# Last attention group finished in halves of its columns, squares of the last two token parts summed on TensorE, order of the last projections and scalings written out by hand

## The chip, the cores and the metric

The kernel runs on one core of one Trainium2 chip. The metric is the device time of one execution in microseconds (us). The engines are named as in the profile: PE is TensorE's matmuls, PEld its weight loads, DVE is VectorE, ACT is ScalarE, POOL is GpSimd, SP is SyncE, which here issues the DMAs. A line such as L1396 is a line of the kernel before; the changed kernel has other line numbers, and its lines stand in the order listings and the diff only.

## The reference

Two layers of a diffusion backbone run over 1024 latent tokens of width 1024, with 256 context tokens ahead of them in the first layer. The first layer is two kinds of grouped attention; the second is a convolution branch beside a neighbourhood attention with a bias table. What this change touches is the end of the second layer: the last heads of the neighbourhood attention, their gate, the output projection, the gated residual, and the final normalization.

```python
def rms_norm(x, g):
    xf = x.astype(jnp.float32)
    y = xf * lax.rsqrt(jnp.mean(xf * xf, axis=-1, keepdims=True) + EPS)
    return (y * g.astype(jnp.float32)).astype(x.dtype)
...
    y_lat = jnp.concatenate([oc, od * jax.nn.silu(dg)], axis=-1) @ w_out     # odd layer
...
        x_lat = x_lat + g_l[:, None, :] * y_lat
...
    return rms_norm(x_lat, final_g)
```

## The kernel before

**Layout.** Everything is held transposed: a tile has 128 channels on its partitions and tokens along its columns. A 1024-channel stream is therefore eight blocks, e = 0 to 7. The latent tokens are dealt into two halves of 512 (hf = 0 and 1). A value that enters a projection is held as a high part and a low part, both in the rounded float type fp32r, and one product is three matmuls into the same PSUM bank: high by high, low by high, high by low (`mm3`, L319, L320, L321). The function `split` makes the two parts: ACT casts the high part (L297), DVE or POOL subtracts (L300).

**Attention of the second layer.** Sixteen groups run one after the other, each one head (hd) over one half of the tokens (hf). A group ends in `attn_gen.flush`: the bank `ov` holds the head's weighted values in partitions 0 to 63 and the softmax denominators in partitions 64 to 127. DVE transposes the denominators of the two halves of 256 columns into `r1` (L421), takes reciprocals (L423), transposes them back and so spreads them (L424), and calls `finish`: two multiplies of 64x256 (L1329), one with the gate over 64x512 (L1331), and for the last head pair the split into `od3`, whose two parts are the moving operands of the last projections (L297 on ACT, L300 on DVE).

**Output projection.** It is accumulated in parts. Channels from the convolution and the first heads are added into `x2[hf]` while the attention still runs. What is left for the end are three token parts, listed in `ENDS`: part 0 is all 512 tokens of half 0, part 1 columns 0 to 255 of half 1, part 2 columns 256 to 511 of half 1. For each part `out1_end(k)` goes through the eight blocks: the matmuls of the last heads (for parts 1 and 2 only the last head pair, f = 7, so one `mm3` of 256 columns), the eviction into x2 with the gated residual on DVE (L1396), and a square on ACT (L1425). In the kernel before the squares of all eight blocks are then added up into two tiles of 128 tokens by columns, on DVE or, where `SQP` says so, on POOL (L1429); for part 2 the two tiles are added (L1432).

**Final norm.** `rstd_steps` sums over the partitions with matmuls whose stationary operand is the summed squares and whose moving operand is a column pair of 1/1024 (`ones`; L252, two per 128 tokens and tile in the program, each of them two passes in the trace). Then come a scalar step on DVE (L255), a power on POOL (L239), three small steps on DVE (L240 to L242), and a matmul against the identity that spreads the result over all partitions (`bc`, L262). `final_norm(k)` scales the eight blocks: those listed in `FNP[k]` by ACT (gain, L1444) and POOL (L1445, from a copy of `bc` that ACT makes, L1440), the others by one DVE instruction (L1447). After each second block SP issues a DMA to the output (L1449).

**Order.** Every engine takes its instructions strictly in the order written. That order is set when the kernel is built, by a scheduler with priorities that goes by the order in which the Python code emits the work. Up to the last group, the ends are woven between attention steps (`weave`). After it, `run(ends(EVS))` emits part 1, its rstd, part 2, norm 1, rstd 2, norm 2, and the scheduler interleaves them. `BUFS` gives the PSUM banks; after the attention (`solo`) projections rotate over four banks (two of `pp`, two of `mx`), so the fifth projection waits until the first was evicted.

Of the kernel before, what the change touches and what calls it, by code (L numbers as in the profile page):

```python
# [56 lines left out]
WV = (73, 53, 77, 24, 12)  # L57
SQ = (0, 1)
EV0 = "e0 c0 f0".split()
EVS = "e1 c1 e2 f1 c2 f2".split()  # L60
NEV = 30
ADDS = (0, 0, 1)
# [26 lines left out]
def tile_kernel(ctx: ExitStack, tc: tile.TileContext, a, out):  # L89
# [152 lines left out]
        VE.scalar_tensor_tensor(r[:, :n], t[:, :n], 1.5, r[:, :n], op0=ALU.add, op1=ALU.mult)  # L242
        return r

    def rstd_steps(pool, accs, n, tag, inv=1.0, tr="tr"):


        nb = n // P
        tr = bank(tr, nm("trs"))
        for b in range(nb):  # L250
            for k, acc in enumerate(accs):
                PE.matmul(tr[:, 2 * b : 2 * b + 2], acc[:, b * P : (b + 1) * P], ones, start=(k == 0),  # L252
                          stop=(k == len(accs) - 1))
        v = pool.tile([P, 8], F32, tag="rbv", name=nm("rbv"), bufs=2)
        VE.tensor_scalar(v[:, :nb], tr[:, 0 : 2 * nb].rearrange("p (b two) -> p b two", two=2)[:, :, 0],  # L255
                         inv, EPS, op0=ALU.mult, op1=ALU.add)
        r = newton_rsqrt(pool, v[:, :nb], nb, "rb")
        yield
        yield
        bc = bank(tag, nm("bc"))  # L260
        for b in range(nb):
            PE.matmul(bc[:, b * P : (b + 1) * P], r[:, b : b + 1].broadcast_to([P, P]), ident, start=True, stop=True)  # L262
        return bc
# [130 lines left out]
    def attn_gen(pool, groups, vshare, look, nexts=None):  # L394
# [6 lines left out]
        def flush():  # L401
            g, t, ph, pl = pend.pop(0)
            k, q0, n, _ = g.tiles[t]
            if t == 0:
                g.ov = bank("ov", nm("ov"))
                if g.load_v is not None:
                    g.load_v()
            V = g.v(k)
            last = t == len(g.tiles) - 1
            o = g.ov[:, q0 : q0 + n]  # L410
            PE.matmul(o, V[:, 64:192], ph[:, :n], start=(t == 0), stop=False)  # L411
            PE.matmul(g.ov[0:64, q0 : q0 + n], V[:, 0:64], ph[:, :n], start=False, stop=False)  # L412
            pvs.append(PE.matmul(o, V[:, 64:192], pl[:, :n], start=False, stop=(last and g.sink is None)))  # L413
            if last:
                if g.sink is not None:
                    PE.matmul(g.ov, g.skm(), g.QL[0:76, :], start=False, stop=True)
                r1 = pool.tile([P, 8, 32], F32, tag="r1", name=nm("r1"), bufs=1)
                r8 = pool.tile([P, 8], F32, tag="r8", name=nm("r8"), bufs=2)
                rb = pool.tile([P, 256], F32, tag="rb", name=nm("rb"), bufs=1)
                for e in range(2):  # L420
                    VE.transpose(r1[e * 64 : (e + 1) * 64].rearrange("p a b -> p (a b)")  # L421
                                 .rearrange("p (a q) -> p a q", a=2), g.den(g.ov[64:128, :], e))
                VE.reciprocal(r8, r1[:, :, 0])  # L423
                VE.transpose(rb, r8[:, :, None].broadcast_to([P, 8, 32]))  # L424
                g.finish(g.ov, rb)
# [638 lines left out]
    with ExitStack():  # L1064
# [193 lines left out]
        def group1(gi, hd, hf):  # L1258
# [66 lines left out]
            def finish(ov, rb):  # L1325
                fin[0] += 1
                y = half("y1")
                for k in range(2):
                    VE.tensor_tensor(y[ds, k * 256 : (k + 1) * 256], ov[0:64, k * 256 : (k + 1) * 256],  # L1329
                                     rb[k * 64 : (k + 1) * 64, :], op=ALU.mult)  # L1330
                VE.scalar_tensor_tensor(y[ds], y[ds], 0.5, g.gt[ds], op0=ALU.mult, op1=ALU.mult)  # L1331
# [76 lines left out]

        def out1_end(k):

            hf, o, n = ENDS[k]
            accs = []
            for e in range(DK):
                if k == 0:
                    if e % 2 == 0:
# [3 lines left out]
                    yield from out1((7,), e, hf, *wend[e // 2], o, n)  # L1419
                x = x2[hf][:, e, o : o + n]  # L1420
                if k:
                    sq = dpool.tile([P, 512], F32, tag="ph" if e in SQ else "pl", name=nm("sq2"), bufs=LOOK1 + 1)[:, :n]
                else:
                    sq = half("sq2", "hf") if e in SQ else pair("sqt", 512, "vT")[:, 0].bitcast(F32)
                SC.activation(sq, x, AF.Square)  # L1425
                if e in SQ:
                    accs.append(sq)
                else:
                    (GP if e in SQP[k] else VE).tensor_tensor(accs[e % 2], accs[e % 2], sq, op=ALU.add)  # L1429
                yield  # L1430
            if ADDS[k]:
                VE.tensor_tensor(accs[0], accs[0], accs[1], op=ALU.add)  # L1432
                accs = accs[:1]
            sums[k] = accs

        def final_norm(k, bc):
            hf, o, n = ENDS[k]
# [17 lines left out]
        def ends(evs):  # L1455
            for ev in evs:
# [1 line left out]
                if ev[0] == "e":  # L1458
                    yield from out1_end(k)
                elif ev[0] == "c":  # L1460
                    bcs[k] = yield from rstd_steps(dpool, sums[k], ENDS[k][2], BCT[k])
                else:
                    yield from final_norm(k, bcs[k])

# [128 lines left out]
```

## Time and profile before

| what | value |
|---|---|
| runs | 1596.81, 1595.64, 1587.97 us; median 1595.64 us |
| profiled execution, its own time | 1590.95 us |
| its span (first to last instruction) | 1589.2 us, so 1.75 us lie around it |
| mean granted TensorE clock | 0.965 |
| busy share | PE 92%, PEld 74%, DVE 71%, ACT 48%, POOL 52% |
| last matmul of the last group (`ov`) ends | 1554.4 us after the start of the span |
| from there to the end of the span | 34.8 us, of which PE is busy 17.86, DVE 24.59, ACT 9.88, POOL 17.50 |

All times inside the span are counted from its start. A row of stretches gives, for each engine, the busy time and the number of instructions, and after them the granted TensorE clock (1.00 is full speed). In a row of the timeline stand the start, the length, the engine, the line, the operation and its operands; several equal instructions in a row are merged, with xN behind them. Matmuls are pipelined: the length of one is more than the distance to the next.

### The profile page before, as it was taken

To read this page: it belongs to the slowest core of one execution; us is meant where nothing else is said; L and a number is where in the kernel's file an instruction comes from. 1 tells how busy PE (TensorE), PEld (TensorE's weight loads), DVE (VectorE), ACT (ScalarE), POOL (GpSimd) and SP (SyncE) were. 2 spreads that over 40 slices of the span, in tenths; PEclk is the share of its full clock that TensorE was granted. 3 is DMA by queue.
4 is the path that set the end of the run, shared out by engine and by line. 5 is a ranking of instruction groups with operands and counts; after the bars stand their busy time and mean duration, and the time that the engine had idled before them with its cause. 6 is when DMAs were issued, how large, how long until landed. Compare 5 with 4: busy or idle time off the path is not lost.

```text
span 1589.2 us, 22236 instructions
## 1 busy us (share of the span) xinstructions
PE 1459.0 (92%) x6984; PEld 1180.6 (74%) x6984; DVE 1124.1 (71%) x2172; ACT 756.6 (48%) x1542; POOL 831.3 (52%) x760
## 2 busy tenths in 40 slices
PE   6789989998999988989999889999999999789895
PEld 1779867787778667767887768888887787577685
DVE  4898787588857668455478776999846467576676
ACT  2722353444434664654555564443433455545473
POOL 1561364455636667756654655754532334444575
PEclk9999999998999999989999989999999999799997
DMA  9548234532442123471111122213456878888732
GB/s 316 179 144 270 83 101 138 176 95 80 146 143 75 36 65 113 156 223 51 57 40 44 57 66 79 92 55 107 162 176 219 246 222 262 239 219 232 221 97 106
DMA packets 198462, 222.01 MB, mean 140 GB/s; under 512 B 18812, under 2 KB 154696, under 8 KB 198344
## 3 DMA queue, kind: packets, MB, share of 16 engines
q1 hardware_dynamic: 191680, 209.02, 42.9%
q10 hardware_dynamic: 6664, 11.57, 2.4%
q8 instruction: 55, 0.90, 0.2%
q14 instruction: 63, 0.52, 0.1%
HBM read 160.49 MB, written 60.03 MB: 139 GB/s over the span
## 4 chain that ended last, share of the span: by engine, by line
PE 61%; DVE 15%; DMA 13%; issue 4%; POOL 3%; SPq 2%; ACT 1%; DVEq 0%; POOLq 0%; ACTq 0%
PE p L320 6%; PE p L319 6%; PE p L321 6%; PE ov L411 4%; PE ov L413 4%; PE ov L412 3%; PE po L320 3%; PE po L319 3%; PE po L321 3%; PE st L448 3%; PE st L452 3%; DMA mw<-in_mod_w_dram 3%; DMA QH<-QD 2%; PE pq L321 2%; PE pq L319 2%
## 5 line engine op out<-in xcount | busy, mean ns | idle before, releaser
L300 POOL TENSOR_TENSOR pl<-pf,ph 128x512 fp32r<-128x512 f32 (+4 forms) x321 | 394.1, 1239 | 304.4 <-ACT ph L297 252.4
L300 POOL TENSOR_TENSOR wl<-wr,wh 128x256 fp32r<-128x256 f32 (+2 forms) x256 | 199.3, 794 | 218.2 <-ACT wh L297 209.4
L460 ACT ACTIVATE pf<-st 128x512 f32<-128x512 f32 x284 | 166.2, 596 | 171.3 <-PE st L452 126.5
L297 ACT CAST ph<-pf 128x512 fp32r<-128x512 f32 (+4 forms) x364 | 209.9, 588 | 38.4 <-PE ov L412 22.0
L297 ACT CAST wh<-wr 128x256 fp32r<-128x256 f32 (+2 forms) x264 | 103.4, 404 | 162.4 <-DMA wr<-in_od_d_dram 38.6
L319 PE MATMUL p<-hh,wh 128*128 128x512 f32 x448 | 177.2, 397 | 2.4 <-DVE spk L300 1.4
L320 PE MATMUL p<-hl,wh 128*128 128x512 f32 x448 | 178.4, 399 | 0.4 <-POOL hl L300 0.4
L321 PE MATMUL p<-hh,wl 128*128 128x512 f32 x448 | 173.3, 396 | 0.2 <-POOL wl L300 0.2
L411 PE MATMUL ov<-ph,Vt 128*128 128x512 f32 (+4 forms) x364 | 144.8, 398 | 15.4 <-DVE y L602 8.2
L413 PE MATMUL ov<-pl,Vt 128*128 128x512 f32 (+4 forms) x364 | 144.5, 397 | 7.5 <-POOL pl L300 5.5
L448 PE MATMUL st<-QH,KAt 128*128 128x512 f32 (+4 forms) x364 | 142.5, 393 | 5.4 <-ACT pf L460 3.4
L412 PE MATMUL ov<-ph,Vt 128*64 128x512 f32 (+4 forms) x364 | 142.0, 390 | 0.0
L452 PE MATMUL st<-QL,KBt 68*128 68x512 f32 (+4 forms) x364 | 137.5, 387 | 0.7 <-DVE QL L390 0.7
L1081 DVE SCALAR_TENSOR_TENSOR cps<-U,taps,cps 128x512 f32<-128x512 f32 x184 | 124.3, 747 | 0.0
L565 DVE TENSOR_REDUCE mp<-mx 128x1 f32<-128x512 f32 x128 | 85.9, 683 | 49.7 <-PE mx L564 49.1
L220 DVE SCALAR_TENSOR_TENSOR macc<-mw,csil,macc 128x512 f32<-128x512 f32 x107 | 93.1, 889 | 23.5 <-DMA mw<-in_mod_w_dram 21.4
L319 PEld LDWEIGHTS p<-hh,wh 128*128 128x128 f32 x448 | 84.1, 188 | 23.4 <-DVE spk L300 1.6
L321 PEld LDWEIGHTS p<-hh,wl 128*128 128x128 f32 x448 | 84.4, 189 | 20.5 <-POOL wl L300 0.6
L320 PEld LDWEIGHTS p<-hl,wh 128*128 128x128 f32 x448 | 84.2, 188 | 19.5 <-POOL hl L300 0.8
L411 PEld LDWEIGHTS ov<-ph,Vt 128*128 128x128 f32 x364 | 71.9, 197 | 32.9 <-issue 8.6
L413 PEld LDWEIGHTS ov<-pl,Vt 128*128 128x128 f32 x364 | 71.6, 197 | 31.5 <-POOL pl L300 8.5
L321 PE MATMUL pq<-wh,hl 128*128 128x384 f32 x256 | 88.7, 348 | 1.1 <-DVE hl L311 0.7
(276 smaller groups left out, 3521.5 us busy)
## 6 DMA issues: line engine op xcount, KB each, us to landing
mw<-in_mod_w_dram SPq DMA_DIRECT2D x34, 512.0 KB, 5.6
Q<-qs SPq DMA_DIRECT2D x40, 256.0 KB, 2.7
QH<-Q SPq DMA_DIRECT2D x80, 128.0 KB, 2.8
wr<-in_od_d_dram SPq DMA_DIRECT2D x64, 128.0 KB, 2.9
mw<-in_mod_w_dram SPq DMA_DIRECT2D x28, 256.0 KB, 3.3
wr<-in_ev_qkv_dram SPq DMA_DIRECT2D x32, 192.0 KB, 3.4
KAt<-KD SPq DMA_DIRECT2D x16, 384.0 KB, 6.1
wr<-in_od_wo_dram SPq DMA_DIRECT2D x48, 128.0 KB, 3.0
```

The costliest lines, as they stand in the source:

```text
L297: SC.copy(hi, src)
L300: (GP if leng == "g" else VE).tensor_tensor(lo, src, hi.bitcast(F32), op=ALU.subtract)
L319: PE.matmul(o, lh, rh, start=first, stop=False)
L320: PE.matmul(o, lh, rl, start=False, stop=False)
L321: done[0] = PE.matmul(o, ll, rh, start=False, stop=last)
L411: PE.matmul(o, V[:, 64:192], ph[:, :n], start=(t == 0), stop=False)
L412: PE.matmul(g.ov[0:64, q0 : q0 + n], V[:, 0:64], ph[:, :n], start=False, stop=False)
L413: pvs.append(PE.matmul(o, V[:, 64:192], pl[:, :n], start=False, stop=(last and g.sink is None)))
L448: sts.append(PE.matmul(st[:, :n], KA[:, cs], g.QH[:, q0 : q0 + n], start=True, stop=False))
L452: PE.matmul(st[:, :n], KB[0:68, cs], g.QL[0:68, q0 : q0 + n], start=False, stop=True)
L460: SC.activation(pf[:, :n], st[:, :n], AF.Exp, scale=1.0 if g.bias else SCALE)
L1081: VE.scalar_tensor_tensor(pc, uc, w, pc, op0=ALU.mult, op1=ALU.add)
```

## The change

Only instructions behind the last attention group move, apart from three things: a tile `zero` of 128x128 is filled once by POOL ahead of the second layer's attention; three scalings of part 0 by the gain, which ACT did during the last group, are gone; and one PSUM bank that part 0's norm uses has another name.

- The last group finishes by halves of 256 columns: transpose, reciprocal, transpose, multiply, gate and split of columns 0 to 255 come ahead of the multiply of columns 256 to 511.
- For parts 1 and 2 no squares are added on DVE or POOL. Each block's square is itself the stationary operand of two matmuls against `ones` that accumulate in one bank, `sums[k]`. A matmul of zeros opens the bank, and `add(4)` holds the matmuls of a block back until four later blocks are squared.
- Part 0's scalings are POOL 4 and DVE 4 instead of 7 and 1; part 2's are POOL 2 and DVE 6 instead of 1 and 7; part 1's stay at 4 and 4.
- The events of `EVS` are replaced by calls in a fixed order: part 1, two blocks of part 2, the rest of part 1's sums, its rstd, four blocks of part 2, norm 1, the rest of part 2, norm 2.

```diff
-BCT = ("mx", "st", "mx")
-FNP = ((0, 1, 2, 3, 4, 5, 6), (0, 2, 4, 6), (6,))
-SQP = ((2, 3, 4, 5, 6), (), (4, 6))
+BCT = ("st", "ov", "mx")
+FNP = ((0, 2, 4, 6), (0, 2, 4, 6), (4, 6))
+SQP = ((2, 3, 4, 5, 6),)
...
+                if g is groups[-1] and layer[0]:
+                    for e in range(2):
+                        es = slice(e * 64, (e + 1) * 64)
+                        VE.transpose(r1[es].rearrange("p a b -> p (a b)").rearrange("p (a q) -> p a q", a=2),
+                                     g.den(g.ov[64:128, :], e))
+                        VE.reciprocal(r8[es], r1[es, :, 0])
+                        VE.transpose(rb[es], r8[es, :, None].broadcast_to([64, 8, 32]))
+                        g.finish(g.ov, rb, (e,))
+                    return
...
+        zero = dpool.tile([P, P], F32, tag="zero", name="zero")
+        GP.memset(zero, 0.0)
...
-                VE.scalar_tensor_tensor(y[ds], y[ds], 0.5, g.gt[ds], op0=ALU.mult, op1=ALU.mult)
+                VE.scalar_tensor_tensor(y[ds, cs], y[ds, cs], 0.5, g.gt[ds, cs], op0=ALU.mult, op1=ALU.mult)
                 if i == 3:
-                    split(y[ds], od3[hf][ds, 0], od3[hf][ds, 1], "s", "v")
+                    split(y[ds, cs], od3[hf][ds, 0, cs], od3[hf][ds, 1, cs], "s", "v")
...
+            if k:
+                sums[k] = bank(("tr", "st")[k - 1], nm("trs"))
+                PE.matmul(sums[k][:, 0 : 2 * n // P], zero, mhalf[:, 0 : 2 * n // P], start=True, stop=False)
+
+            def add(m):
+
+                while len(waiting) > m:
+                    e, sq = waiting.pop(0)
+                    for b in range(n // P):
+                        PE.matmul(sums[k][:, 2 * b : 2 * b + 2], sq[:, b * P : (b + 1) * P], ones,
+                                  start=False, stop=(e == DK - 1 and b == n // P - 1))
...
                 if k:
-                    sq = dpool.tile([P, 512], F32, tag="ph" if e in SQ else "pl", name=nm("sq2"), bufs=LOOK1 + 1)[:, :n]
...
+                    sq = dpool.tile([P, 512], F32, tag=("ph", "pl")[e % 2], name=nm("sq2"), bufs=LOOK1 + 1)[:, :n]
+                    SC.activation(sq, x, AF.Square)
+                    waiting.append((e, sq))
+                    add(4)
...
-        run(ends(EVS))
+        e1, e2 = out1_end(1), out1_end(2)
...
+        go1(e1, DK)
+        go1(e2, 2)
+        run(e1)
+        bc1 = rstd_steps(dpool, None, ENDS[1][2], BCT[1], sums=sums[1])
+        next(bc1)
+        go1(e2, 4)
+        run(final_norm(1, run(bc1)))
+        run(e2)
+        run(final_norm(2, run(rstd_steps(dpool, None, ENDS[2][2], BCT[2], sums=sums[2]))))
```

The order on PE where part 1 passes into part 2, in the kernel before. `po` is the bank of one projection, `od` the split attention output, `wh` and `wl` the two parts of the weights:

```order
L319 MATMUL po_4255_16624<-od_3646_14558,wh_16574 128x256
L320 MATMUL po_4255_16624<-od_3646_14558,wh_16574 128x256
L321 MATMUL po_4255_16624<-od_3646_14558,wl_16575 128x256
L319 MATMUL po_4264_16656<-od_3646_14558,wh_16556 128x256
L320 MATMUL po_4264_16656<-od_3646_14558,wh_16556 128x256
L321 MATMUL po_4264_16656<-od_3646_14558,wl_16557 128x256
L319 MATMUL po_4266_16663<-od_3646_14558,wh_16556 128x256
L320 MATMUL po_4266_16663<-od_3646_14558,wh_16556 128x256
L321 MATMUL po_4266_16663<-od_3646_14558,wl_16557 128x256
```

The same place in the changed kernel. `trs` is the bank `sums[1]` and `sq` a block's squares; `x2` are the two halves of 128 tokens, and each of these matmuls is two passes in the trace:

```order
L1437 MATMUL trs_16582<-ones,sq_4251_16610 128x2 x2
L317 MATMUL po_4261_16650<-od_3646_14560,wh_16560 128x256
L318 MATMUL po_4261_16650<-od_3646_14560,wh_16560 128x256
L319 MATMUL po_4261_16650<-od_3646_14560,wl_16561 128x256
L1437 MATMUL trs_16582<-ones,sq_4253_16617 128x2 x2
L317 MATMUL po_4263_16657<-od_3646_14560,wh_16560 128x256
L318 MATMUL po_4263_16657<-od_3646_14560,wh_16560 128x256
L319 MATMUL po_4263_16657<-od_3646_14560,wl_16561 128x256
L317 MATMUL po_4268_16680<-od_3646_14560,wh_16566 128x256
```

Between two projections of three matmuls stand now two matmuls with two columns each, that is four passes; nothing else stands there, and the projections themselves are as they were.

The end of PE's program, in the kernel before. `trs` is the bank of the sums, `bc` the spread result:

```order
L252 MATMUL trs_16640<-ones,sq_4244_16583 128x2
L319 MATMUL po_4278_16710<-od_3646_14558,wh_16574 128x256
L320 MATMUL po_4278_16710<-od_3646_14558,wh_16574 128x256
L321 MATMUL po_4278_16710<-od_3646_14558,wl_16575 128x256
L252 MATMUL trs_16640<-ones,sq_4246_16590 128x2
L252 MATMUL trs_16640<-ones,sq_4244_16583 128x2
L252 MATMUL trs_16640<-ones,sq_4246_16590 128x2
L252 MATMUL trs_16737<-ones,sq_4265_16661 128x2 x2
L262 MATMUL bc_16653<-ident,nr_16647 128x128 x2
L262 MATMUL bc_16748<-ident,nr_16742 128x128 x2
```

And in the changed kernel:

```order
L318 MATMUL po_4280_16742<-od_3646_14560,wh_16578 128x256
L319 MATMUL po_4280_16742<-od_3646_14560,wl_16579 128x256
L1437 MATMUL trs_16648<-ones,sq_4269_16685 128x2 x2
L1437 MATMUL trs_16648<-ones,sq_4271_16692 128x2 x2
L1437 MATMUL trs_16648<-ones,sq_4273_16699 128x2 x2
L1437 MATMUL trs_16648<-ones,sq_4275_16708 128x2 x2
L260 MATMUL bc_16712<-ident,nr_16674 128x128 x2
L1437 MATMUL trs_16648<-ones,sq_4279_16738 128x2 x2
L1437 MATMUL trs_16648<-ones,sq_4281_16747 128x2 x2
L260 MATMUL bc_16767<-ident,nr_16761 128x128 x2
```

Part 2's sums stand now behind its projections, block by block, and part 1's `bc` stands ahead of the last two blocks of part 2's sums, which before came behind all of part 2's work. From the first block of part 1's sums on, PE's program holds 16 blocks of four such passes; before it held 12 passes of this kind for the two parts.

POOL's end, in the kernel before. `nr` is the power of L239, `bcs` the copy of `bc`:

```order
L239 TENSOR_TENSOR nr_16503<-rbv_16501,mhalf 128x4
L1445 TENSOR_TENSOR x_3643_14555<-x_3643_14555,bcs_16517 128x512 x7
L1429 TENSOR_TENSOR sq_4265_16661<-sq_4265_16661,sq_4273_16691 128x256
L1429 TENSOR_TENSOR sq_4265_16661<-sq_4265_16661,sq_4277_16707 128x256
L239 TENSOR_TENSOR nr_16647<-rbv_16645,mhalf 128x2
L239 TENSOR_TENSOR nr_16742<-rbv_16740,mhalf 128x2
L1445 TENSOR_TENSOR x_3645_14557<-x_3645_14557,bcs_16719 128x256 x4
L1445 TENSOR_TENSOR x_3645_14557<-x_3645_14557,bcs_16751 128x256
```

And in the changed kernel:

```order
L237 TENSOR_TENSOR nr_16505<-rbv_16503,mhalf 128x4
L1476 TENSOR_TENSOR x_3643_14557<-x_3643_14557,bcs_16519 128x512 x4
L237 TENSOR_TENSOR nr_16674<-rbv_16672,mhalf 128x2
L1476 TENSOR_TENSOR x_3645_14559<-x_3645_14559,bcs_16715 128x256 x4
L237 TENSOR_TENSOR nr_16761<-rbv_16759,mhalf 128x2
L1476 TENSOR_TENSOR x_3645_14559<-x_3645_14559,bcs_16770 128x256 x2
```

Part 2's additions are gone from POOL; the power for part 2, the second `nr` with 128x2, stood ahead of part 1's four scalings and stands now behind them.

More of the change, by code (lines that the diff above doesn't have):

```diff
@@ L243, in newton_rsqrt, with rstd_steps @@
         return r
-    def rstd_steps(pool, accs, n, tag, inv=1.0, tr="tr"):
+    def rstd_steps(pool, accs, n, tag, inv=1.0, tr="tr", sums=None):
         nb = n // P
-        tr = bank(tr, nm("trs"))
-        for b in range(nb):
+        tr = bank(tr, nm("trs")) if sums is None else sums
+        for b in range(nb if sums is None else 0):
             for k, acc in enumerate(accs):
@@ L1430, in out1_end @@
                 yield
[L1431 to L1434, printed above, removed]
+            if k:
+                add(0)
+            else:
+                sums[k] = accs
         def final_norm(k, bc):
@@ L1460, in ends @@
                 elif ev[0] == "c":
-                    bcs[k] = yield from rstd_steps(dpool, sums[k], ENDS[k][2], BCT[k])
+                    bcs[k] = yield from rstd_steps(dpool, sums[k], ENDS[k][2], BCT[k], sums=sums[k] if k else None)
                 else:
```

24 lines of the change are left out of this document (15 added, 9 removed).

## The prediction

> **What bounds the kernel now.** I read the page first, then the tail by stretches of 3.4 us, then its timeline and its groups by shape. The order listings show that nothing but the end moves, so the page serves to say how much that is.
>
> ```profile
> span 1589.2 us, 22236 instructions
> PE 1459.0 (92%) x6984; PEld 1180.6 (74%) x6984; DVE 1124.1 (71%) x2172; ACT 756.6 (48%) x1542; POOL 831.3 (52%) x760
> PEclk9999999998999999989999989999999999799997
> ```
>
> PE is busy for 92% of the span at nearly full clock, so PE bounds the whole; the last digit of the clock row, 7, is the slice of the last 40 us and shows that the end is another stage. Here are stretches of it, and two from an early place that I need below. The columns are: stretch, its length, busy time and count of PE, PEld, DVE, ACT and POOL, the granted clock, DMA.
>
> ```profile
> 108.20:111.60 3.40, 3.40 (x19) 3.40 (x18) 3.37 (x6) 0.91 (x3) 1.12 (x1) 0.50 0.91 309
> 111.60:115.00 3.40, 3.40 (x13) 2.91 (x13) 3.40 (x6) 1.46 (x4) 2.22 (x2) 0.50 0.62 198
> ...
> 1552.10:1555.50 3.40, 3.40 (x25) 2.92 (x23) 2.39 (x5) 0.63 (x1) 1.31 (x2) 1.00 0.01 2
> 1555.50:1558.90 3.40, 0.84 (x7) 0.76 (x7) 2.34 (x7) 0.61 (x1) 1.53 (x1) 1.00 0.02 5
> 1558.90:1562.30 3.40, 2.63 (x13) 2.35 (x13) 2.01 (x6) 0.98 (x3) 0.00 (x0) 0.50 0.00 0
> 1562.30:1565.70 3.40, 3.40 (x18) 3.40 (x18) 2.13 (x4) 1.77 (x4) 2.11 (x2) 0.50 0.00 0
> 1565.70:1569.10 3.40, 2.82 (x20) 2.41 (x19) 3.40 (x8) 1.88 (x6) 3.40 (x4) 1.00 0.40 154
> 1569.10:1572.50 3.40, 1.24 (x6) 0.83 (x6) 3.40 (x7) 1.60 (x5) 3.40 (x3) 1.00 0.40 154
> 1572.50:1575.90 3.40, 2.53 (x11) 2.47 (x11) 3.40 (x8) 2.12 (x6) 1.42 (x3) 0.51 0.81 308
> ```
>
> Two things are to be seen. From 1565.7 to 1575.9 DVE is busy in all of each stretch: the tail is bound by DVE, while PE has gaps. And the clock goes by these stretches: it falls to half behind one in which PE worked 0.84 of 3.40 us, comes back behind 1562.30:1565.70, which is full of matmuls, holds with 2.82 and falls again behind 1.24.
>
> **The change part by part.** First the head, from the end of `ov` to the first low part.
>
> ```profile
> 1554.47 0.92 DVE L421 STREAM_TRANSPOSE r<-ov 64x256 f32<-64x256 f32 x2 [0.20 <-PE ov L413]
> 1555.43 0.20 DVE L423 RECIPROCAL r<-r 128x8 f32<-128x8 f32 x1
> 1555.66 0.45 DVE L424 STREAM_TRANSPOSE rb<-r 128x256 f32<-128x256 f32 x1
> 1556.14 0.85 DVE L1329 TENSOR_TENSOR y<-ov,rb 64x256 f32<-64x256 f32 x2
> 1557.03 0.16 DVE L255 TENSOR_SCALAR rbv<-trs 128x4 f32<-128x4 f32 x1
> 1557.22 0.69 DVE L1331 SCALAR_TENSOR_TENSOR y<-y,gt 64x512 f32<-64x512 f32 x1
> 1557.94 0.61 ACT L297 CAST od<-y 64x512 fp32r<-64x512 f32 x1 [4.39 <-DVE y L1331]
> 1559.22 0.69 DVE L300 TENSOR_TENSOR od<-y,od 64x512 fp32r<-64x512 f32 x1
> 1559.96 0.58 PE L320 MATMUL po<-od,wh 128*128 128x256 f32 x1 [0.77 <-DVE od L300]
> ```
>
> Before, the low part lets PE go on at 1559.96. After, DVE does for the first half a transpose 0.46, reciprocal 0.20, transpose 0.45, multiply 0.42, then the other half's transpose 0.46, `rbv` 0.16, the gate (0.42, as the 64x256 multiply), reciprocal and transpose 0.65, and the low part 0.42: 3.64 us, with ten hand-overs of 0.04 us (1554.47 + 0.92 to 1555.43) 4.0, so at 1558.5. ACT's cast runs beside the second reciprocal. That is 1.5 us earlier, but little comes of it: the second half's multiply, gate and two small steps (1.3 us) stand on DVE ahead of the first eviction, so the first bank of four is free at about 1560.2, and the fifth projection starts then. From there PE's program is the path. Its prices:
>
> ```profile
> 1554.33 1.72 PE L252 MATMUL trs<-ones,sq 128*128 128x2 f32 x14
> ...
> 1562.90 0.41 PE L320 MATMUL po<-od,wh 128*128 128x256 f32 x1
> ...
> 1565.25 0.41 PE L319 MATMUL po<-od,wh 128*128 128x256 f32 x1
> ...
> 1577.52 0.98 PE L252 MATMUL trs<-ones,sq 128*128 128x2 f32 x4 [1.59 <-DVE sq L1432]
> 1578.36 1.20 PE L262 MATMUL bc<-ident,nr 128*128 128x128 f32 x4
> ```
>
> At half clock 11 passes of 256 columns lie between 1562.90 and 1565.25, 0.213 us each; the two-column passes of the sums take as much, (1578.36 - 1577.52) / 4 = 0.21, and so do those of `bc`. At full clock a sum's pass takes 1.72 / 14 = 0.12, or 0.115 without the last one's tail. So a block of the changed program (three wide passes, four narrow) costs PE 1.49 us at half clock and 0.8 at full, where it cost 0.64 and 0.35.
>
> From the fifth projection to the end of part 2's sums PE has 3 passes of that projection, 8 of part 0's `bc`, 2 of zeros, 11 projections of 3, 64 of sums and 4 of part 1's `bc`: 114. At half clock they take 24.3 us, to 1584.8 with 0.3 for the first and the last.
>
> Is it half? The early place speaks for it. By line, L226 alone (the same two-column shape) has there:
>
> ```profile
> 108.20:111.60 3.40, 1.19 (x7) 1.40 (x7) 0.50 0.91 309
> ```
>
> So PE was busy all 3.40 us, 1.19 of it with two-column passes, and the clock did not come back behind it; with wide passes alone it did at 1565.7. In the changed program four of seven passes are narrow. The stretch 1555.50:1558.90 will hold a handful of passes more than before, and I take it that the clock still falls there. The Trainium skill, "TensorE: Matmul & The Clock Gate", Part 1 (the HAM clock gate), says that the clock is released after about 3.4 us of sustained matmul activity and names no width of the matmuls. By that sentence the clock would be full at the latest two stretches after 1560.2, and the sum would come to about -2 us in place of +6; the row of 108.20 differs from it.
>
> What follows the sums, and what leaves DVE and POOL:
>
> ```profile
> L1445 POOL TENSOR_TENSOR x<-x,bcs 128x512 f32<-128x512 f32 x7 | 9.4, 1383 | 4.8 <-PE po L321 4.8
> L1429 DVE TENSOR_TENSOR sq<-sq,sq 128x256 f32<-128x256 f32 x10 | 7.4, 758 | 0.0
> L1396 DVE SCALAR_TENSOR_TENSOR x<-po,modT,x 128x256 f32<-128x256 f32 x16 | 7.1, 473 | 2.6 <-PE po L321 2.6
> L1447 DVE SCALAR_TENSOR_TENSOR x<-x,fg,bc 128x512 f32<-128x512 f32 x1 | 0.7, 740 | 0.0
> L1440 ACT COPY bcs<-bc 128x256 f32<-128x256 f32 x2 | 0.7, 372 | 4.9 <-PE bc L262 4.9
> ...
> 1578.78 0.70 POOL L239 TENSOR_TENSOR nr<-rbv,mhalf 128x2 f32<-128x2 f32 x1 [1.37 <-DVE rbv L255]
> 1580.05 3.45 POOL L1445 TENSOR_TENSOR x<-x,bcs 128x256 f32<-128x256 f32 x5 [0.58 <-ACT bcs L1440]
> ...
> 1580.11 1.22 PE L262 MATMUL bc<-ident,nr 128*128 128x128 f32 x4 [0.55 <-DVE nr L242]
> ...
> 1580.01 4.61 DVE L1447 SCALAR_TENSOR_TENSOR x<-x,fg,bc 128x256 f32<-128x256 f32 x11
> ...
> 1580.80 4.99 SPq L1449 DMA_DIRECT2D out_dram<-x  x8
> ```
>
> DVE loses ten additions, 7.4 us, and the last one (L1432), and gains three scalings of 0.74: 5 us less work on what was the bound. That is the whole gain the change can have, and PE takes it: DVE's 16 evictions (7.1) and four scalings (3.0) fit easily into 24.3 us, so they cost nothing unless PE is at full clock.
>
> At the end, part 1's `bc` is 8 passes (1.7 us) ahead of the last sum, at 1583.1. POOL waits for its copy (0.37), does four scalings (3.45 / 5 = 0.69 each) to 1586.3, and only then the power for part 2, which now stands behind them: 1587.0, while its input is there at 1585.0. Three small DVE steps 0.6, `bc` 1.25, six scalings of 4.61 / 11 = 0.42: 1591.4. The last DMA issue (4.99 / 8 = 0.62) ends at 1592.1, against 1580.80 + 4.99 = 1585.8 before: **+6.3 us**. The landing behind it stays as it is.
>
> At no cost: bank names (the banks are free when asked for), the three gain multiplications that leave ACT (PE bounds there). The fill of `zero` is one small instruction ahead of the second attention; bounds 0 and, as the nearest row, one power of 0.70; I take 0. Part 2's second POOL scaling runs beside DVE's six.
>
> **The rivals.** *The full clock comes back* (because a stretch happens to begin near 1560, where 13 passes of projection and `bc` nearly fill it, or because narrow passes count as well). 13 passes at half clock end at 1563.1, 101 at 0.115 take 11.6; with 1.7 for a stretch that falls back, since narrow work leaves little wide, the sums end at 1576.4 and the last issue 7.3 later, at 1583.7: -2.1 us. For it speaks 1562.30:1565.70, against it 108.20:111.60. The stretches can lie otherwise in each run. *The clock never falls*: 114 passes at 0.115 from 1560.2 end at 1573.4, and the chain behind `bc` (8.3 from 1572.5) ends at 1580.8: -5.0 us. Against it: PE has hardly any work from 1554.4 to 1558.5. *Each block's weights are loaded only when its square is there*, on PE between the projections. One row prices it:
>
> ```profile
> L252 PEld LDWEIGHTS trs<-ones,sq x28: 186/192/337, 1553.6 to 1578.1; 128*128 128x128 f32 x28
> ```
>
> If each of 16 blocks shows its first load of up to 0.337 us, 5.4 us come on top: +11.7 us, slower by 0.7%. It decides if squares arrive as PE asks for them; for it speaks that ACT also has gain multiplications and a copy in its queue, against it that `add(4)` leaves four blocks between, 6 us at half clock.
>
> **How the numbers follow.** The profiled execution took 1590.95 us, 4.7 under the median of 1595.64; the four times of before spread over 8.8 us, with a mean of 1592.8. The forecast stands on that mean: 1592.8 + 6.3, about 1599 (1597.3 by the profiled execution alone). Chances: forecast 0.48, clock comes back 0.28 (1590.7 on the mean), clock never falls 0.09 (1587.8), late loads 0.15 (1604.5). The range goes from 1587, the second and third with the profiled execution's lower start, to 1604. A measurement of this kernel can tell about 0.5%, 8 us, from no change. Over that on the slow side come a third of the forecast (it needs 1.7 us of the spread) and most of the late loads: 0.27. On the fast side a third of the never-falling clock and a seventh of the returning one: 0.07. The rest, 0.66, is within.
>
> **What would show it.** Right: stretches from 1562 to 1585 with a clock of 0.50 and PE busy throughout, narrow passes 0.21 us apart, DVE with gaps, the last power on POOL behind four scalings, last issue near 1592. Wrong: a clock of 1.00 there, with PE waiting for evictions; or PE waiting at the sums for ACT's squares; or any difference ahead of 1554.

## The result and the profile after

Median of 22 runs each: 1597.56 us after (1591.03 to 1607.75), 1596.14 us before (1587.97 to 1602.41). The ratio is 1.0009, 95% interval 0.9994 to 1.0025: +1.4 us, between -1 and +4. That is no change that can be measured, and the forecast of 1599.0 stands 1.4 us off. A second comparison, below, gave 0.9975 (0.9956 to 0.9993), so the sign is not settled.

The profiled execution of the changed kernel took 1607.19 us, the second longest of its 22. From its page:

```profile
span 1604.5 us, 22331 instructions
PE 1473.5 (92%) x7040; PEld 1194.6 (74%) x7040; DVE 1122.7 (70%) x2167; ACT 756.8 (47%) x1541; POOL 825.5 (51%) x757
PEclk9999989999999999989999989999999999899995
```

The span is 15.3 us longer, but 11.8 of that lie ahead of the tail, where both kernels have all but the same instructions: the last matmul into `ov` ends at 1566.20 instead of 1554.44. Over all traces of this study that point lies between 1547.6 and 1566.2. So I compare tails, counted from the end of `ov`. By stretches (same columns as before: stretch, length, busy time and count of PE, PEld, DVE, ACT, POOL, granted clock, DMA), the tail of the changed kernel is:

```profile
1565.40:1568.80 3.40, 2.64 (x21) 2.31 (x19) 3.00 (x8) 0.00 (x0) 0.20 (x1) 1.00 0.02 5
1568.80:1572.20 3.40, 2.90 (x15) 2.81 (x15) 3.15 (x12) 1.29 (x4) 1.06 (x1) 0.50 0.00 0
1572.20:1575.60 3.40, 3.40 (x18) 3.40 (x18) 1.82 (x5) 3.08 (x8) 0.17 (x1) 0.50 0.00 0
1575.60:1579.10 3.50, 3.50 (x31) 3.50 (x32) 3.50 (x7) 0.69 (x3) 3.50 (x3) 0.99 0.41 156
1579.10:1582.50 3.40, 3.40 (x18) 3.40 (x18) 2.03 (x5) 2.22 (x7) 1.33 (x2) 0.50 1.00 379
1582.50:1585.90 3.40, 3.40 (x17) 3.40 (x18) 1.19 (x4) 1.60 (x4) 0.70 (x1) 0.50 0.21 80
1585.90:1589.30 3.40, 3.40 (x18) 3.40 (x18) 1.20 (x4) 1.34 (x3) 0.00 (x0) 0.50 0.00 0
1589.30:1592.70 3.40, 3.40 (x17) 3.40 (x18) 0.23 (x1) 0.37 (x1) 0.18 (x1) 0.50 0.00 0
1566.20:1604.50 38.30, 27.30 (x146) 26.74 (x146) 19.92 (x54) 10.97 (x27) 11.79 (x13) 0.58 0.31 110
```

DVE, which was busy in all of 1565.7 to 1575.9 before, now has gaps everywhere but in one stretch; PE is busy without a break from 1572.2 to 1592.7. The bound has moved from DVE to PE, as forecast. In five of those six stretches the clock is 0.50 although PE is full. One stretch, 1575.60:1579.10, has the full clock, and 31 passes instead of 17 or 18 are recorded in it.

The end of the same tail, from the timeline (start, length, engine, line, operation):

```profile
1592.52 2.77 POOL L1476 TENSOR_TENSOR x<-x,bcs 128x256 f32<-128x256 f32 x4 [7.61 <-ACT bcs L1471]
...
1592.75 0.78 PE L1437 MATMUL trs<-ones,sq 128*128 128x2 f32 x3
1592.87 1.26 DVE L1478 SCALAR_TENSOR_TENSOR x<-x,fg,bc 128x256 f32<-128x256 f32 x3
1593.27 8.13 SPq L1480 DMA_DIRECT2D out_dram<-x  x8
1594.05 0.15 DVE L253 TENSOR_SCALAR rbv<-trs 128x2 f32<-128x2 f32 x1
1595.25 0.69 POOL L237 TENSOR_TENSOR nr<-rbv,mhalf 128x2 f32<-128x2 f32 x1
...
1596.59 1.22 PE L260 MATMUL bc<-ident,nr 128*128 128x128 f32 x4 [3.06 <-DVE nr L240]
1597.85 0.37 ACT L1471 COPY bcs<-bc 128x256 f32<-128x256 f32 x1 [5.41 <-PE bc L260]
1598.25 2.44 DVE L1478 SCALAR_TENSOR_TENSOR x<-x,fg,bc 128x256 f32<-128x256 f32 x6 [1.72 <-ACT bcs L1471]
```

The power for part 2 (L237) starts when POOL's four scalings are through, 1.05 us behind its input. From the last sum (1592.75 + 0.78 = 1593.53) to the end of the last issue (1593.27 + 8.13 = 1601.40) it takes 7.87 us, where it took 7.30 before.

### The profile page after: what moved, and what is told of

Its sections match the earlier page's. It is cut to its first block, busy times and chain, and to the rows that moved or that the text cites. A ratio compares the mean times of both kernels' runs of the same rounds, so it can differ in the third digit from the quotient of the medians.

```text
span 1604.5 us, 22331 instructions
## 1 busy us (share of the span) xinstructions
PE 1473.5 (92%) x7040; PEld 1194.6 (74%) x7040; DVE 1122.7 (70%) x2167; ACT 756.8 (47%) x1541; POOL 825.5 (51%) x757
## 4 chain that ended last, share of the span: by engine, by line
PE 62%; DVE 14%; DMA 11%; issue 5%; POOL 4%; SPq 2%; ACT 1%; DVEq 0%; POOLq 0%; ACTq 0%
PE p L318 6%; PE p L319 6%; PE p L317 6%; PE po L317 4%; PE ov L409 4%; PE po L318 4%; PE po L319 4%; PE ov L411 4%; PE ov L410 4%; PE st L455 3%; PE st L459 3%; DMA mw<-in_mod_w_dram 2%; DMA QH<-QD 2%; PE pq L319 2%; PE pq L318 2%
```

## Experiments

The theory was: PE bounds the changed tail, because two-column passes occupy it as long as wide ones and do not hold its clock. The rivals: the clock counts all passes, or the order at the end sets the time.

The table gathers what the traces show, in us behind the end of `ov`: where the clock first falls, how many stretches at full clock come behind that until the last sum, where the last sum and the last DMA issue end.

| kernel and trace | first fall | full stretches later | last sum | last issue |
|---|---|---|---|---|
| before, first | 4.5 | 2 | 24.06 | 31.36 |
| before, e6 | 3.7 | 2 | 24.09 | 31.39 |
| changed, first | 2.6 | 1 | 27.33 | 35.20 |
| changed, e10 | 3.3 | 2 | 25.86 | 33.72 |
| changed, e5 | 4.1 | 3 | 21.81 | 29.66 |
| changed with probe, e1 | 11.8 | 0 | 26.78 | 34.63 |
| with filler, e2 | 4.5 | 1 | 25.84 | 33.13 |
| halves alone, e7 | 2.9 | 2 | 25.66 | 34.61 |
| no sums on PE, e4 | 2.7 | 3 | 21.46 | 28.76 |
| no sums on PE, e11 | 3.5 | 2 | 21.02 | 28.32 |
| one narrow pass, e8 | 4.5 | 2 | 20.77 | 29.78 |
| one narrow pass, e12 | 3.0 | 2 | 21.75 | 30.47 |
| squares as moving operand, e3 | 2.4 | 3 | 18.86 | 27.51 |
| squares as moving operand, e9 | 11.7 | 2 | 19.12 | 27.77 |

**Do narrow passes count for the clock?** Added behind the last norm, on PE alone:

```diff
+        for n_, w_ in ((56, 2), (16, 256), (56, 2)):
+            for _ in range(n_):
+                PE.matmul(pb[:, :w_], b_[:, 0:P], ones if w_ == 2 else b_[:, 0:w_], start=True, stop=True)
```

> This kernel does all that the changed kernel does and then, on PE alone, more: 56 narrow fp32 matmuls (128x2, 112 passes), 16 wide ones (256 columns), 56 narrow ones again. Its total time is not to be compared; what counts is the clock of each stretch of 3.4 us. Theory (two-column passes do not count as work for the clock): the first narrow run starts at a clock of 0.50 and stays there to its end, 112 x 0.213 = 24 us; the clock rises one or two stretches into the wide run; the second narrow run starts at 1.00 and falls to 0.50 within two stretches, so that it takes over 18 us as well. Rival (any gapless matmul work counts, whatever its width): the clock rises within two stretches of the first narrow pass, so that the first narrow run takes about 16 us (32 passes at 0.213 in two stretches, 80 at 0.115), and the second stays at 1.00 and takes 12.9 us.

The timeline gives the three runs, the stretches their clock:

```profile
1592.62 24.06 PE L1532 MATMUL prb<-ones,bcs 128*128 128x2 f32 x112 [0.46 <-ACT bcs L1473]
1616.53 9.21 PE L1532 MATMUL prb<-bcs 128*128 128x256 f32 x32
1625.58 18.99 PE L1532 MATMUL prb<-ones,bcs 128*128 128x2 f32 x112
```

```profile
1596.80:1600.20 3.40, 3.40 (x18) 3.40 (x17) 0.00 (x0) 0.00 (x0) 0.00 (x0) 0.50 0.20 72
...
1610.50:1613.90 3.40, 3.40 (x17) 3.40 (x17) 0.00 (x0) 0.00 (x0) 0.00 (x0) 0.50 0.00 0
1613.90:1617.30 3.40, 3.40 (x15) 3.31 (x16) 0.00 (x0) 0.00 (x0) 0.00 (x0) 0.50 0.02 5
1617.30:1620.70 3.40, 3.40 (x10) 2.68 (x9) 0.00 (x0) 0.00 (x0) 0.00 (x0) 0.50 0.00 0
1620.70:1624.10 3.40, 3.40 (x18) 2.99 (x17) 0.00 (x0) 0.00 (x0) 0.00 (x0) 1.00 0.00 0
1624.10:1627.50 3.40, 3.40 (x26) 3.22 (x25) 0.00 (x0) 0.00 (x0) 0.00 (x0) 1.00 0.00 0
1627.50:1631.00 3.50, 3.50 (x34) 3.50 (x33) 0.00 (x0) 0.00 (x0) 0.00 (x0) 0.99 0.00 0
1631.00:1634.40 3.40, 3.40 (x17) 3.40 (x18) 0.00 (x0) 0.00 (x0) 0.00 (x0) 0.50 0.00 0
```

The first 112 narrow passes take 24.06 us, 0.215 each, at 0.50 throughout with PE full. The clock rises behind the first stretch of wide passes (1617.30). In the second narrow run it stays up behind a stretch that was part wide, and falls behind 1627.50:1631.00, which held 34 narrow passes and no others. So the theory is shown and the rival refuted: a stretch full of two-column passes does not bring the clock back (six such stretches in a row in the first run) and does not hold it (seen once). The wide passes of the probe are fp32 like the narrow ones, so the width is what differs. The Trainium skill, "TensorE: Matmul & The Clock Gate", Part 1 (the HAM clock gate), ties the release to sustained matmul activity of about 3.4 us. For these passes the rows above differ from it over seven such times, and the measurement decides.

**Cover the gap in the head.** Six matmuls of 512 columns behind `ov`:

```diff
+                    for _ in range(6):
+                        PE.matmul(fb, pl[:, 0:P], pl, start=True, stop=True)
```

> The changed kernel with six matmuls of 512 columns more, on data that is already there, behind the last ov matmul on PE, 2.2 us of full-clock work in the gap of the head; their output is not used. Measure: from the end of the last ov matmul to the end of the span, 38.3 us in the changed kernel (here ov's end means the last ov matmul, not the filler). Theory (half clock on PE is what costs the tail): the clock does not fall in the gap, holds at 1.00 at least 6 us longer than in the changed kernel's trace (there until 2.6 us behind ov's end), and the tail is 33 to 36.5. Rival (the tail's length is set by the order, the power behind four scalings and what follows, and by ACT and DVE, whatever the clock): the clock is 1.00 longer, but the tail stays within 37.3 to 39.3.

The tail was 36.48 us, just inside the theory's range, but the clock fell at 4.5 us and not later than 8.6 as expected. The tail lies within what the unchanged kernel shows by itself (32.7 to 38.3), so this run tells nothing apart. The six matmuls filled 1.4 us behind `ov`, not the 2.2 expected. Nor are they all that differs: the scheduler moved part 0's `bc` to 12.6 us behind `ov` (it starts at 5.8 to 6.6 in the traces of the changed kernel), and part 2's power ahead of POOL's scalings of part 1, so that the chain behind the last sum is 7.30 us.

**Squares as the moving operand.** One pass of 256 columns per block, in fp32r, in place of four narrow ones; the row of sums is copied by ACT and transposed by PE:

```diff
-                    for b in range(n // P):
-                        PE.matmul(sums[k][:, 2 * b : 2 * b + 2], sq[:, b * P : (b + 1) * P], ones,
-                                  start=False, stop=(e == DK - 1 and b == n // P - 1))
+                    PE.matmul(sums[k][0:2, :n], onesr, sq, start=(e == 0), stop=(e == DK - 1))
...
+            SC.copy(row, sums[0:2, :n])
+            tr = sums[:, 256 : 256 + 2 * nb]
+            for b in range(nb):
+                PE.transpose(tr[:, 2 * b : 2 * b + 2], row[:, b * P : (b + 1) * P], ident[0:2, 0:2])
```

> The changed kernel, but the squares (in fp32r) are the moving operand: one pass of 256 columns per block against a 128x2 stationary of 1/1024 in place of four two-column passes; the sums come out as a row, which ACT copies and PE transposes twice per part before the scalar steps. Theory (PE's passes bound the tail, and two-column passes keep its clock down): PE has 46 passes less; at half clock that is 9.8 us, and wide passes alone bring the clock back for at least two stretches; the tail, 38.3 in the changed kernel, becomes 28.5 to 33, and DVE (16 evictions of 0.47 and seven or more scalings) and the added copy and transposes (about 1.2 us per part) set its end. Rival (the order written by hand and the chain at the end set it): the tail stays above 36.5.

The tail was 30.59 us, in the theory's range and 4.1 below the kernel before. By stretches, the two behind the return of the clock (same columns):

```profile
1568.20:1571.60 3.40, 2.13 (x18) 1.71 (x16) 3.24 (x6) 0.73 (x2) 3.40 (x3) 1.00 0.32 120
1571.60:1575.00 3.40, 3.07 (x25) 2.78 (x26) 3.40 (x10) 3.03 (x10) 1.61 (x2) 1.00 1.02 380
```

The clock is up and PE is no longer full: 2.13, then 3.07 of 3.40 us, while DVE is busy for 3.24 and 3.40. PE has ceased to be the bound. The second trace (e9) lies quite differently, with its first fall at 11.7 instead of 2.4, and its last issue differs by only 0.3 us. Here, too, the scheduler put the power for part 2 ahead of part 1's scalings, but the gain is not from there: the chain behind the last sum is longer than in the changed kernel, 8.65 us instead of 7.87.

**Undo the sums alone.** Halves, order and shares as the change writes them, squares added on DVE and POOL. The sums of both parts are 12 passes again, one matmul of two passes for each 128 tokens and tile:

```diff
-SQP = ((2, 3, 4, 5, 6),)
+SQP = ((2, 3, 4, 5, 6), (), (4, 6))
...
-        bc1 = rstd_steps(dpool, None, ENDS[1][2], BCT[1], sums=sums[1])
+        bc1 = rstd_steps(dpool, sums[1], ENDS[1][2], BCT[1])
```

> The changed kernel with its halves, its order and its shares of the scalings, but the squares of parts 1 and 2 added on DVE and POOL as in the kernel before: the sums on PE alone are undone. Theory (the sums on PE cost the tail, and DVE's relief is all they bring): PE has 56 passes less, 11.9 us at half clock, DVE and POOL the additions again (7.4 us and more); the tail is 33.5 to 36, about that of the kernel before (34.7). Rival (the order by hand costs it: power for part 2 behind POOL's four scalings): the tail is 37.5 to 40, since the order is kept and DVE has its additions again.

32.13 us, 1.4 below even the theory's range. The clock's first fall (2.7) lies where it lay in the first trace of the changed kernel (2.6), so the two compare well: at this position the difference is 35.20 - 28.76 = 6.4 us. But the order at the end was not kept, as the rival had assumed: the scheduler put the power for part 2 ahead of POOL's scalings. From POOL's timeline:

```profile
1577.10 0.89 POOL L237 TENSOR_TENSOR nr<-rbv,mhalf 128x2 f32<-128x2 f32 x1
1579.35 0.70 POOL L237 TENSOR_TENSOR nr<-rbv,mhalf 128x2 f32<-128x2 f32 x1 [1.37 <-DVE rbv L253]
1580.62 4.14 POOL L1460 TENSOR_TENSOR x<-x,bcs 128x256 f32<-128x256 f32 x6 [0.57 <-ACT bcs L1455]
```

So this run alone doesn't rule the rival out, but its rows bound it. Behind the last sum it is 7.30 us here and 7.87 in the changed kernel, 0.6 of the 6.4. The other 5.9 lie ahead of the last sum (27.33 - 21.46); that is what the sums on PE cost at this position. A second pair at like positions, e10 and e11 (3.3 and 3.5), both from one comparison, gives 33.72 - 28.32 = 5.4, again with 0.6 of it behind the last sum.

**The same two kernels again.**

> The changed kernel itself once more, unchanged, for another position of the 3.4 us stretches of the clock against the end of ov. Measure: from ov's end to the end of the span, 38.3 us in its first trace. Theory (PE at half clock through the sums, and the tail varies with where the stretches begin): 36 to 40, sums' stretches full of passes at 0.50 with at most one or two stretches at 1.00 among them; each stretch at 1.00 more or less moves the end of part 2's sums by about 14 passes x 0.213 = 3 us. Rival (the forecast as it stood, no stretch at full clock, is the usual case and the first trace an exception): 41 to 42.

> The kernel before once more, unchanged, for the same purpose; its tail from ov's end was 34.7 us. Theory (this tail is bound by DVE for most of its length, so the clock's stretches matter little): 33.7 to 35.7. Rival (the position of the stretches moves it as much as the changed kernel's): outside of that, as far as 32 or 37.

The changed kernel's tail was 32.74 us, 5.5 below its first trace, with not one instruction different. That is outside both ranges. Its tail by stretches:

```profile
1561.90:1565.30 3.40, 2.14 (x17) 1.97 (x18) 3.18 (x10) 0.40 (x1) 1.26 (x1) 1.00 0.02 5
1565.30:1568.70 3.40, 3.40 (x17) 3.32 (x17) 3.22 (x10) 2.44 (x7) 0.00 (x0) 0.50 0.00 0
1568.70:1572.10 3.40, 3.40 (x32) 3.40 (x31) 2.19 (x4) 1.58 (x4) 2.15 (x2) 1.00 0.00 0
1572.10:1575.50 3.40, 3.11 (x27) 3.02 (x27) 3.32 (x8) 2.41 (x8) 2.85 (x3) 1.00 0.98 369
1575.50:1578.90 3.40, 3.40 (x33) 3.40 (x31) 2.40 (x8) 2.63 (x8) 0.69 (x1) 1.00 0.66 250
1578.90:1582.40 3.50, 3.50 (x18) 3.50 (x19) 0.48 (x2) 0.59 (x2) 0.43 (x1) 0.51 0.00 0
```

One half-clock stretch, filled by projections and `bc`, brings the clock back at once, and it holds for three stretches. In the first trace the stretch from 1568.80 was only 2.90 full, a second one at half clock was needed, and the clock held for one. Before's second trace had 34.76 (34.72 in the first), but its first fall was only 0.7 us off, so how far before depends on the position stays open.

**Halves alone, on the kernel before.**

```diff
+                if g is groups[-1] and layer[0]:
+                    for e in range(2):
...
+                        g.finish(g.ov, rb, (e,))
+                    return
```

> The kernel before with the first part of the change alone: the last group finished in halves of columns; the squares are added on DVE and POOL, and the order and the shares of scalings are those of before. Theory (the first low part is ready 1.5 us earlier but the fifth projection waits for the first eviction at about 5.7 us behind ov's end, against 5.5 to 6 before; so halves alone give little): tail 34 to 35.2, against 34.7 of the kernel before. Rival (the 2.6 us by which the kernel without the sums on PE was shorter than before come from the halves): 31.8 to 33.

37.47 us: worse than either expected. The low part was indeed early (first projection at 3.26 instead of 4.17), but the scheduler now put part 1's norm ahead of part 2's, on DVE and on POOL. From the timeline of this kernel:

```profile
1581.72 1.66 DVE L1461 SCALAR_TENSOR_TENSOR x<-x,fg,bc 128x256 f32<-128x256 f32 x4 [1.38 <-ACT bcs L1454]
1583.29 0.15 DVE L255 TENSOR_SCALAR rbv<-trs 128x2 f32<-128x2 f32 x1
...
1581.76 2.77 POOL L1459 TENSOR_TENSOR x<-x,bcs 128x256 f32<-128x256 f32 x4 [2.17 <-ACT bcs L1454]
1584.49 0.70 POOL L239 TENSOR_TENSOR nr<-rbv,mhalf 128x2 f32<-128x2 f32 x1
```

DVE does `rbv`, and POOL the power, only behind its four scalings. From the last sum to the last issue it took 34.61 - 25.66 = 8.95 us instead of 7.30: 1.65 us for that order. Another 1.6 us were lost before the last sum, and the same trace shows a like order there:

```profile
1577.94 0.96 POOL L239 TENSOR_TENSOR nr<-rbv,mhalf 128x2 f32<-128x2 f32 x1 [1.19 <-ACT sq L1439]
1578.87 0.72 POOL L1443 TENSOR_TENSOR sq<-sq,sq 128x256 f32<-128x256 f32 x1
...
1579.92 0.42 DVE L1446 TENSOR_TENSOR sq<-sq,sq 128x256 f32<-128x256 f32 x1
```

POOL does part 1's power ahead of its last addition of squares for part 2, and DVE adds the two tiles only behind that and part 1's three small steps. This addition ends 24.08 us behind `ov` and ended at 22.93 before. PE then does part 1's `bc` first, so that part 2's sums start at 24.81 instead of 23.08. What the halves give in the order of before is not shown.

Against e4 at nearly the same position (28.76), order and shares by hand save 5.9 us, of which 3.2 only make good what this order lost. Against the kernel before, e4 stands at -2.6. So in the first trace the change contains a saving of 2.6 us (halves, order and shares) and a loss of 6.4 (sums on PE and what they move); together that is its +3.8.

**Half the narrow passes.** Squares and `ones` in fp32r (`onesr`):

```diff
-                        PE.matmul(sums[k][:, 2 * b : 2 * b + 2], sq[:, b * P : (b + 1) * P], ones,
+                        PE.matmul(sums[k][:, 2 * b : 2 * b + 2], sq[:, b * P : (b + 1) * P], onesr,
```

> The changed kernel with squares and the column pair of 1/1024 in fp32r, so that each of the 32 two-column matmuls of the sums may be one pass instead of two; their width, place and order are kept. Theory (the number of passes on PE at half clock is what the tail pays): 32 passes less, each 0.213 us at half clock, 6.8 us less PE work; the clock does not come back more often than in the changed kernel by this (narrow passes stay narrow), the sums end 4 to 7 us earlier and the tail is 32 to 35, from 38.3. Rival (a pass costs by its weight load, which is no shorter in fp32r, or the chain at the end decides): the tail is above 36.5.

Tail 32.86 us, in the theory's range; but e5, the changed kernel itself at a like position (first fall 4.1, here 4.5), had 32.74, so the tail alone shows nothing. The pair e10 and e12 (3.3 and 3.0) shows more: last issue at 33.72 and 30.47. The order is not quite kept: part 0's `bc` stands here ahead of the fifth projection, in the changed kernel behind it. Groups by shape, first the changed kernel (first trace), then this one:

```profile
L1437 PE MATMUL trs<-ones,sq 128*128 128x2 f32 x64 | 12.0, 301 | 0.0
```

```profile
L1439 PE MATMUL trs<-onesr,sq 128*128 128x2 f32 x32 | 4.9, 243 | 0.0
```

64 passes have become 32, and 12.0 us of PE 4.9. A part of that is the clock: in e5, where it was up for longer, the 64 passes took 9.2. The chain behind the last sum is longer here (9.0), so not all of it shows at the end.

**Timed against before**, in one comparison with 24 runs of before (median 1596.55):

> The kernel with the squares as moving operand (one pass of 256 columns per block) again, now timed against the kernel before over many runs, so that the position of the clock's stretches averages out. Theory (its PE work is short and wide, so that no position of the stretches makes PE the bound): last DMA issue 27 to 29 us behind ov's end at any position, against 31.4 before, so the ratio is 0.997 to 0.9985 (2.5 to 4.5 us less). Rival (its one trace lay well, as one of the changed kernel's did): ratio 0.999 to 1.001.

> The changed kernel itself, in the same comparison. Theory (its tail depends on where the stretches begin: last issue seen 35.2, 34.6 and 29.7 us behind ov's end, against 31.4 before; mean of the three +1.8): ratio 1.000 to 1.002, and its trace here has a last issue between 29.5 and 36. Rival (the position that gave 29.7 is the usual one): ratio 0.9985 to 0.9995.

> Halves, hand order and shares of scalings, squares added on DVE and POOL as before, timed. Theory (at one and the same position of the stretches its last issue came 28.8 us behind ov's end, the changed kernel's 35.2 and that of halves alone 34.6; over all positions the sums on PE cost a part of this): last issue 28 to 32, ratio 0.998 to 0.9995, below the changed kernel's in this comparison by 1 to 6 us. Rival (the sums cost nothing on the mean over positions): the ratio is that of the changed kernel within 1 us.

> The changed kernel with one narrow pass per matmul of the sums instead of two, timed. Theory (what the tail pays is PE passes at half clock; with 32 passes less PE is the bound only where the clock stays low throughout): last issue 28 to 31, ratio 0.997 to 0.9995, below the changed kernel's by 2 to 6 us. Rival (its one trace lay well): the ratio is that of the changed kernel within 1 us.

| kernel | median us | runs | ratio to before | last issue in its trace |
|---|---|---|---|---|
| squares as moving operand (e9) | 1590.29 | 7 | 0.9948 (0.9922 to 0.9975) | 27.77 |
| changed (e10) | 1594.44 | 12 | 0.9975 (0.9956 to 0.9993) | 33.72 |
| no sums on PE (e11) | 1595.24 | 12 | 0.9977 (0.9953 to 1.0000) | 28.32 |
| one narrow pass (e12) | 1590.17 | 6 | 0.9939 (0.9917 to 0.9961) | 30.47 |

The last issues are within the theory's ranges in all four; the ratios are all lower than expected. For the changed kernel neither range was met: by the ratio it is 4 us faster here (2.1 by the medians) and 1.4 slower in the first comparison, and the two intervals do not meet, while its four traces average 33.30 for the last issue, 1.9 above before. The tails cannot give 4 us of gain on the mean, and the start of the tail varies by 18.6 us between traces, so I take the difference between the comparisons for the scatter of the part ahead; that is argued, not shown.

For e11 it was the rival's condition that came true: its time is the changed kernel's within 1 us (0.8 longer by the medians, the ratio higher by 0.0002), although its two tails are 4.8 us shorter on average. So the cost of the sums on PE is shown in the tails and not in the timed runs. Two kernels, e9 and e12, stand below the changed one by 4.2 and 4.3 us in the same comparison, and below before by 6.3 and 6.4 (medians). Their tails account for 3.6 to 3.9 and 0.9 to 1.6 us of that; the rest is not explained. It is of the size by which the two comparisons of the changed kernel differ (5.4 us by the ratios), so how much of it is real stays open.

## Why the prediction was right, point by point

**The bound moves from DVE to PE; DVE's 5 us stay hidden.** Right in the first trace: DVE busy 19.92 of 38.30 us, PE full through the sums.

**Head by halves.** Right in time, not in cause. The low part was forecast at 1558.5 and ready 3.67 us behind `ov`, which is 1558.1 in before's count; its first matmul starts at 1558.7, behind the four with the high part. The fifth projection was forecast at 1560.2 and started at 1560.4, but not, as forecast, when the first eviction freed its bank: that was over 5.42 us behind `ov`, at 1559.9, and PE at half clock came through the first four projections, without a gap, only at 1560.4.

**Narrow passes cost 0.21 us and do not bring the clock back.** Right, and shown by the probe (0.215 us; 0.50 over all of the first run).

**"At half clock they take 24.3 us, to 1584.8."** This is the term that was mis-sized: 30.4 us behind `ov`, measured 27.33, 25.86, 21.81 and 26.78. No trace had the half clock all the way. A stretch at half clock holds 3.40 / 0.213 = 16 passes, one at full clock 3.40 / 0.115 = 30, so each full stretch behind the fifth projection takes 14 x 0.213 = 3.0 us off: 27.4 for one (measured 27.33), 24.4 for two (e10: 25.86, where PE waited 0.6 us for evictions), 21.4 for three (21.81). What failed is the step from "narrow passes don't bring it back" to "it stays half": the projections and `bc` passes ahead of the sums brought it back in the first trace, e5 and e10, and once up, mixed stretches can hold it (e5, 1572.10:1575.50). How many narrow passes a stretch may contain is not shown: at half clock with PE full, 12 wide and 4 narrow passes brought it back in the first trace (1572.20:1575.60) and did not in e2 (1569.90:1573.30).

**The rival that the clock comes back** was no alternative but another position of the same kernel: it put the sums' end at 1576.4, 22.0 behind `ov`, and the end at -2.1 us; e5 shows 21.81 and 29.66 - 31.36 = -1.7. It named the reason as well (where a stretch begins). One chance each for two cases was the wrong form: e5 is nearly the rival's case, the other three traces lie between the two, and the forecast's own case, half clock all the way, is in none of them.

**The clock never falls.** Its ground was wrong, that PE's idle head must make the clock fall: in e1 it held for the first 11.8 us. Its gain did not come either: PE waited 1.7 us for evictions, then the clock fell in the sums, and the last issue came at 34.63, where the rival had -5.0 against before.

**Late weight loads.** Did not come: PE has no idle time ahead of the sums (0.0 in their group above).

**The end.** 7.3 us from the last sum to the last issue forecast, 7.85 to 7.87 in all four traces. The power behind four scalings was forecast 1.3 us behind its input and came 1.05 behind it. Not counted were the copy by ACT, 0.4, and 0.2 until that power starts (1.72 us behind the last sum, forecast 1.5). `rbv`, which stands 0.5 behind the last sum and DVE's scalings, adds nothing, since the power waits for POOL.

**The sum.** +6.3 forecast; +3.8, +3.3, +2.4 and -1.7 in four traces, +1.4 in the first comparison. That the number of 1599 came so close is luck, since two errors cancel: the base of 1592.8 was 3.3 too low (before's 22 runs have 1596.14), the effect 4.9 too high. That no difference would be measurable is right for the first comparison; the sign stays open.

## What to carry over

Before moving a reduction to the tensor engine, count its passes and not its columns: a 128x2 fp32 matmul cost two passes here, each as long at half clock (0.213 us) as a 256-column fp32r pass of the projections, and a stretch made of them lost the clock. The same sum with the data as the moving operand is one wide pass and had the shortest tail here. A stage of some 35 us that PE bounds, and whose clock goes by stretches of 3.4, has no single time: take several traces, and compare those in which the stretches lie alike. And read the order in each of them: in five of the six variants here, all but the probe, the scheduler moved other work as well.

## What was not expected of the hardware

- The same instructions took 32.7 to 38.3 us in the tail, by where the clock's stretches began.
- Small DVE steps were longer beside POOL's scalings. In e3, beside four scalings on POOL, each of the three steps on 128x2 took about 0.65 us; the same steps for part 1, with POOL idle, took 0.16, as they did behind the scalings in the changed kernel. No run tested this by itself. Timeline of e3:

```profile
1576.27 0.16 DVE L238 TENSOR_TENSOR nt<-nr,rbv 128x2 f32<-128x2 f32 x1 [0.81 <-POOL nr L237]
...
1578.82 2.76 POOL L1480 TENSOR_TENSOR x<-x,bcs 128x256 f32<-128x256 f32 x4
...
1579.61 0.63 DVE L238 TENSOR_TENSOR nt<-nr,rbv 128x2 f32<-128x2 f32 x1
1580.27 0.65 DVE L239 SCALAR_TENSOR_TENSOR nt<-nt,nr 128x2 f32<-128x2 f32 x1
1580.95 0.65 DVE L240 SCALAR_TENSOR_TENSOR nr<-nt,nr 128x2 f32<-128x2 f32 x1
```
